# w2 of expert 5 loaded in two halves and w2 of expert 7 in 8, 4 and 4 rows, with the second products in the same pieces

## The chip, the cores and the metric

The kernel runs on one core of a Trainium2 chip. The metric is the device time of one execution in microseconds (us). Four runs of the kernel before gave 181.62 to 182.16 us, with a median of 181.73 us.

## The reference

Eight experts each apply a two-layer network to their own 256 tokens. x is 8 x 256 x 512, w1 is 8 x 512 x 2048, w2 is 8 x 2048 x 512, all float32; b1 and b2 are the biases.

```
h = np.matmul(x, w1) + b1[:, np.newaxis, :]
h = np.maximum(h, 0)
return (np.matmul(h, w2) + b2[:, np.newaxis, :]).astype(np.float32)
```

## The kernel before, in words

Everything is loaded into SBUF as float16 (the DMAs issued by GpSimd convert on the way) and multiplied by TensorE into float32 sums in PSUM.

**The tiles.** The weights of one expert are one tile each: w1 is 128 partitions x 4 rows x 2048, w2 is 128 partitions x 16 rows x 512 (`nJ` = 16 rows per partition). Each is 2 MB in SBUF and 4 MB in DRAM. Three w1 tiles and three w2 tiles exist at a time (`w1_pool`, `w2_pool`, L48 and L49), so a load waits until the product that used the same buffer three experts ago is done.

**The first product** of an expert (`first_product`, L114 to L136) has 16 blocks of four matmuls each (L121); ScalarE adds b1 and applies the maximum with zero (L128), and writes `hT`. In its middle VectorE transposes x of the next expert (`transposes`, L95).

**The second product** (`second_product`, L166 to L185) begins with two bias matmuls (L171), one for each block of 128 tokens. Then come 32 matmuls (L178), one for each of two token blocks (`tb`) and 16 rows (`j`) of w2, which sum up in the two PSUM tiles `po[0]` and `po[1]`. For the experts in `HALVED` (6 and 7) the 32 go in two halves: rows 0 to 7 for both token blocks, then rows 8 to 15 for both. For the others all 16 rows of one token block come first. `store` (L142) then copies `po[0]` out on VectorE (L156) and `po[1]` on ScalarE (L157).

**The order of the work.** The outer loop (L227) does at step s the first product of expert s and the second product of expert s - 3 (`LAG`). At the end, after the first product of expert 7, the second products of experts 4, 5, 6 and 7 follow each other; the last three have no first products between them. All weight loads are issued by GpSimd (POOL) from one list, `ring` (L215 to L225), in the order in which the products need them, and travel on one queue, q0. `load_w2` (L88 to L93) issues w2 of experts 0 to 5 as one DMA each and that of experts 6 and 7 as two DMAs of eight rows. PE and POOL keep the order in which the program is written (`ordered`).

**The stores.** The results of experts 0 to 3 and of experts 4 and 5 are collected in two group tiles (`GROUPS`) and stored by POOL with `flush` (L138, DMA at L140), behind the last weights on q0: 2 MB for the first group and 1 MB for the second. Expert 6's result is stored in three parts (`PARTS`, L164): rows 0 to 24 and 121 to 127 by SyncE (SP, queue q1), the 96 rows between by ScalarE (ACT, queue q10). Expert 7's result is one store by SP on q1, 0.5 MB.

Of the kernel before, what the change touches and what calls it, by code (L numbers as in the profile page):

```python
# [10 lines left out]
def kernel(  # L11
# [9 lines left out]
    nc = tc.nc  # L21
    fp32 = mybir.dt.float32
    fp16 = mybir.dt.float16
    E, T, H = x.shape
# [4 lines left out]
    nJ = M // P  # L29
# [4 lines left out]


    GROUPS = {0: 4, 4: 2}
    HALVED = (E - 2, E - 1)


    PARTS = {E - 2: ((0, 25, False), (25, 121, True), (121, 128, False))}  # L40
# [3 lines left out]
    def ordered(ins):  # L44
        return tc.keep_in_program_order(ins)
# [20 lines left out]
    w2_sb = [None] * E  # L66
# [2 lines left out]
    results = {}  # L69
    group_of = {first + i: (first, n) for first, n in GROUPS.items() for i in range(n)}  # L70

    def load_x(first, n):

        R = n * T // P
        t = x_pool.tile([P, R, H], fp16, tag=f"x{first}", name=f"x{first}")
        ordered(nc.gpsimd.dma_start(  # L76
            out=t, in_=x[first : first + n].rearrange("e (p r) h -> (e p) r h", r=R)
        ))
        for i in range(n):
            x16[first + i] = (t, i * (P // n), R)  # L80
# [7 lines left out]
    def load_w2(e):  # L88
        src = w2[e].rearrange("(p j) h -> p j h", j=nJ)
        w2_sb[e] = w2_pool.tile([P, nJ, H], fp16, tag="w2", name="w2sb")  # L90
        half = nJ // 2 if e in HALVED else nJ
        for lo in range(0, nJ, half):
            ordered(nc.gpsimd.dma_start(out=w2_sb[e][:, lo : lo + half], in_=src[:, lo : lo + half]))  # L93

    def transposes(e):  # L95

# [45 lines left out]
    def store(e, po):  # L142
        if e in group_of:
            first, n = group_of[e]
            split, rows = n, P // n
            if e == first:
                results[e] = group_pool.tile(
                    [P, split * nTB, H], fp32, tag=f"out{e}", name=f"out{e}")
        else:
            first, n, split, rows = e, 1, 1, P  # L150
            results[e] = out_pool.tile([P, nTB, H], fp32, tag="out", name="out")
        out_sb = results[first]
        at = (e - first) * rows
        for k in range(split):
            part = slice(k * rows, (k + 1) * rows)
            nc.vector.tensor_copy(out=out_sb[at : at + rows, k * nTB, :], in_=po[0][part])  # L156
            nc.scalar.copy(out=out_sb[at : at + rows, k * nTB + 1, :], in_=po[1][part])  # L157
        dst = out[first : first + n].rearrange("e (p r) h -> (e p) r h", r=split * nTB)
        if e in group_of:
            if e == first + n - 1:  # L160
                pending[first] = (dst, out_sb)
            return
        for p0, p1, scalar in PARTS.get(e, ((0, P, False),)):
            (nc.scalar if scalar else nc.sync).dma_start(out=dst[p0:p1], in_=out_sb[p0:p1])  # L164

    def second_product(e):  # L166
        po = []
        for tb in range(nTB):
            t = psum_o.tile([P, H], fp32, tag=f"po{tb}", name=f"po{tb}")
            po.append(t)  # L170
            ordered(nc.tensor.matmul(  # L171
                out=t, lhsT=ones1, rhs=b2_sb[0:1, e * H : (e + 1) * H], start=True, stop=False,
            ))
        half = nJ // 2 if e in HALVED else nJ
        for lo in range(0, nJ, half):
            for tb in range(nTB):
                for j in range(lo, lo + half):
                    ordered(nc.tensor.matmul(  # L178
                        out=po[tb],
                        lhsT=hT[e][:, j, tb * P : (tb + 1) * P],  # L180
                        rhs=w2_sb[e][:, j, :],
                        start=False,
                        stop=(j == nJ - 1),
                    ))
        store(e, po)  # L185

    x32 = []
    for e in range(nXF32):
# [4 lines left out]
        out=b2_sb,  # L193
        in_=b2.rearrange("e h -> (e h)").rearrange("(o f) -> o f", o=1),
# [12 lines left out]
    for b in range(nB):  # L207
        nc.vector.transpose(  # L208
            out=b1T[b * B : (b + 1) * B, nB - 1 - b : nB - 1 - b + nJ * B],
            in_=b1_rows.rearrange("r (i j) -> r j i", j=nJ),  # L210
# [5 lines left out]
    for s in range(1, E + LAG - 1):  # L216
        if s < E:
            if s in X_LOADS:
                ring.append((s - 2, load_x, (s, X_LOADS[s])))
            ring.append((s - 2, load_w1, (s,)))  # L220
        if s >= LAG:
            ring.append((s - 2, load_w2, (s - LAG,)))
    ring.append((E + LAG - 3, load_w2, (E - 1,)))
    for first, n in GROUPS.items():
        ring.append((first + n + LAG, flush, (first,)))  # L225

    for s in range(E + LAG):  # L227
        while ring and ring[0][0] <= s:
            _, put, args = ring.pop(0)
            put(*args)  # L230
        if s < E:
            first_product(s)
        if s >= LAG:
            second_product(s - LAG)
# [31 lines left out]
```

## Time and profile before

| what | value |
|---|---|
| median of four runs | 181.73 us |
| the profiled execution | 181.7 us |
| its span, first to last instruction | 179.9 us |
| mean granted TensorE clock | 0.948 |
| PE (matmuls) busy | 129.0 us, 72% |
| DVE / ACT / POOL busy | 87.8 / 70.6 / 13.5 us |
| moved by DMA, as counted at the destination | 40.56 MB, mean 225 GB/s |
| queue q0 | 38.35 MB, 96.4% of the 16 DMA engines' span |
| read from / written to DRAM | 71.39 / 4.19 MB |
| one w2 DMA of 2 MB, issue to landing | 47.1 us median |
| one w2 DMA of 1 MB, issue to landing | 23.9 us median |
| matmul at L178 | 379 ns median, x256 |

"Span" is the time between the first and last instruction in the trace; the execution's own time is 1.8 us longer. "Issue to landing" is the time from the issuing instruction to the arrival of the last byte; where transfers queue up behind each other it is mostly queueing time. "DMA share" in a stretch of time is the mean busy share of the 16 DMA engines; it can read a little over 1 where packets on one engine overlap. "Granted clock" is the share of TensorE's full clock that the chip allowed in that stretch. The chain of waits is followed back from the last instruction: at each step to what released it. The loads of float32 weights into float16 tiles show up at about half the GB/s of the stores, because bytes are counted at the destination.

### The profile page before, as it was taken

What the parts mean: (1) busy time and instruction counts of PE and PEld (TensorE: products, weight loads), DVE (VectorE), ACT (ScalarE), POOL (GpSimd) and SP (SyncE); (2) the same over time, 40 slices, a digit from 0 to 9 for tenths busy, and PEclk for the clock granted to TensorE, in tenths of its full rate; (3) what the DMA queues carried; (4) which work ended last, traced back from release to release, by engine and by line L of the source; (5) the groups of instructions that cost most, each with busy time, mean ns of one, the idle gap of its engine ahead of it and who ended that gap; (6) DMA issues with size and microseconds to landing.
All of it is one profiled execution on the core that took longest, in us unless ns stands there. A gap on an engine that the chain in (4) does not pass through costs nothing.

```text
span 179.9 us, 1958 instructions
## 1 busy us (share of the span) xinstructions
PE 129.0 (72%) x784; PEld 86.9 (48%) x784; DVE 87.8 (49%) x125; ACT 70.6 (39%) x151; POOL 13.5 (7%) x28
## 2 busy tenths in 40 slices
PE   0006099979599930999769593959499986999960
PEld 0004079979487410794369242934189432434420
DVE  1999931988000199999999998003300020301010
ACT  0000458979477050491279006940549020020010
POOL 7100000220201010001100001000200011010000
PEclk9999999999879996599999999999969997899998
DMA  6999999999999999899999999999998999999995
GB/s 214 252 229 195 233 214 194 233 228 204 213 229 199 213 233 219 189 233 226 219 197 233 219 193 230 229 200 211 233 219 189 233 209 208 217 213 220 358 413 224
DMA packets 3828, 40.56 MB, mean 225 GB/s; under 512 B 460, under 2 KB 476, under 8 KB 1132
## 3 DMA queue, kind: packets, MB, share of 16 engines
q0 software_dynamic: 3232, 38.35, 96.4%
q1 hardware_dynamic: 476, 1.70, 2.5%
q10 hardware_dynamic: 112, 0.39, 0.5%
q8 instruction: 6, 0.10, 0.2%
q14 instruction: 2, 0.02, 0.0%
HBM read 71.39 MB, written 4.19 MB: 420 GB/s over the span
## 4 chain that ended last, share of the span: by engine, by line
DMA 67%; PE 26%; POOL 2%; another core or an unknown queue 1%; issue 1%; ACT 0%; POOLq 0%
DMA w1sb<-in_w_dram 44%; DMA w2sb<-in_w_dram 23%; PE po L178 17%; PE ph L121 8%; PE po L171 1%; POOL w1sb L84 1%; ACT out L157 0%; POOL x L76 0%; POOL b_sb L192 0%; POOL b_rows L196 0%; POOLq L250 0%
## 5 line engine op out<-in xcount | busy, mean ns | idle before, releaser
L121 PE MATMUL ph<-xT,w1sb 128*128 128x256 f16 x512 | 66.6, 298 | 38.1 <-DMA w1sb<-in_w_dram 26.3
L121 PEld LDWEIGHTS <-w1sb 128*128 128x128 f16 x512 | 60.8, 148 | 44.8 <-DMA w1sb<-in_w_dram 36.4
L112 DVE STREAM_TRANSPOSE xT<-x 32x256 f16<-32x256 f16 (+1 forms) x64 | 53.0, 889 | 25.9 <-DMA x<-in_x_dram 18.1
L128 ACT ACTIVATE hT<-ph,b1T 128x256 f16<-128x256 f32 x128 | 56.6, 477 | 19.7 <-PE ph L121 19.5
L178 PE MATMUL po<-w2sb,hT 128*128 128x512 f16 x256 | 58.2, 387 | 6.6 <-DMA w2sb<-in_w_dram 6.6
L178 PEld LDWEIGHTS <-hT 128*128 128x128 f16 x256 | 25.3, 99 | 39.5 <-issue 12.0
L156 DVE COPY out<-po 32x512 f32<-32x512 f32 (+2 forms) x22 | 15.1, 687 | 54.4 <-PE po L178 54.2
L157 ACT COPY out<-po 32x512 f32<-32x512 f32 (+2 forms) x22 | 12.7, 579 | 63.8 <-PE po L178 63.6
L109 DVE STREAM_TRANSPOSE xT<-x 32x256 f16<-32x256 f16 x32 | 13.9, 436 | 0.5
L93 POOL DMA_DIRECT2D w2sb<-in_w_dram x10 | 5.3, 534 | 70.7 <-PE po L178 70.7
L84 POOL DMA_DIRECT2D w1sb<-in_w_dram x8 | 4.9, 612 | 65.2 <-PE ph L121 64.4
L128 ACT ACT_TABLE_LOAD x1 | 1.3, 1283 | 20.2 <-DVE b1T L208 20.2
L171 PE MATMUL po<-b_sb,ones 1*128 1x512 f16 x16 | 4.8, 379 | 0.0
L208 DVE STREAM_TRANSPOSE b1T<-b_rows 32x512 f32<-32x512 f32 x4 | 4.1, 1034 | 0.1
L201 DVE CAST x<-x 128x1024 f16<-128x1024 f32 x2 | 1.4, 694 | 3.2 <-DMA x<-in_x_dram 3.2
L140 POOL DMA_DIRECT2D out_dram<-out x2 | 1.1, 542 | 11.0 <-ACT out L157 11.0
L171 PEld LDWEIGHTS <-ones 1*128 1x128 f16 x16 | 0.9, 92 | 2.1 <-issue 2.1
L76 POOL DMA_DIRECT2D x<-in_x_dram x2 | 1.1, 552 | 0.0
L197 DVE MEMSET ones<- 1x128 f16 x1 | 0.2, 165 | 0.8 <-PEq L250 0.8
L196 POOL DMA_DIRECT2D b_rows<-in_b_dram x1 | 0.5, 515 | 0.0
L192 POOL DMA_DIRECT2D b_sb<-in_b_dram x1 | 0.5, 513 | 0.0
L250 POOL MEMSET const-float32-0.0<- 128x1 f32 x1 | 0.1, 98 | 0.2 <-issue 0.2
(3 smaller groups left out, 0.3 us busy)
## 6 DMA issues: line engine op xcount, KB each, us to landing
w1sb<-in_w_dram POOLq DMA_DIRECT2D x8, 2048.0 KB, 34.3
w2sb<-in_w_dram POOLq DMA_DIRECT2D x6, 2048.0 KB, 47.1
w2sb<-in_w_dram POOLq DMA_DIRECT2D x4, 1024.0 KB, 23.9
out_dram<-out POOLq DMA_DIRECT2D x1, 2048.0 KB, 26.7
x<-in_x_dram SPq DMA_DIRECT2D x2, 512.0 KB, 3.8
x<-in_x_dram POOLq DMA_DIRECT2D x1, 1024.0 KB, 30.2
out_dram<-out POOLq DMA_DIRECT2D x1, 1024.0 KB, 17.6
x<-in_x_dram POOLq DMA_DIRECT2D x1, 512.0 KB, 24.2
```

Of the source, the lines that this page charges most:

```text
L84: ordered(nc.gpsimd.dma_start(out=w1_sb[e], in_=w1[e].rearrange("(p kc) m -> p kc m", kc=nKC)))
L93: ordered(nc.gpsimd.dma_start(out=w2_sb[e][:, lo : lo + half], in_=src[:, lo : lo + half]))
L109: nc.vector.transpose(out=out[:, :, g, :, 0, :], in_=block[:, :, :, 0, :])
L112: nc.vector.transpose(out=out[:, tb, g], in_=block[:, tb])
L121: ordered(nc.tensor.matmul(out=ph, lhsT=w1_sb[e][:, kc, :].rearrange("p (q j) -> p q j", j=nJ)[:, :, j], rhs=xT[e][:, kc, :], start=(kc == 0),
L128: nc.scalar.activation(out=hT[e][:, j, :].rearrange("p (tb k i) -> p tb k i", tb=nTB, k=split), in_=ph.rearrange("p (tb i k) -> p tb k i", ...
L156: nc.vector.tensor_copy(out=out_sb[at : at + rows, k * nTB, :], in_=po[0][part])
L157: nc.scalar.copy(out=out_sb[at : at + rows, k * nTB + 1, :], in_=po[1][part])
L171: ordered(nc.tensor.matmul(out=t, lhsT=ones1, rhs=b2_sb[0:1, e * H : (e + 1) * H], start=True, stop=False,))
L178: ordered(nc.tensor.matmul(out=po[tb], lhsT=hT[e][:, j, tb * P : (tb + 1) * P], rhs=w2_sb[e][:, j, :], start=False, stop=(j == nJ - 1),))
L201: nc.vector.tensor_copy(out=t, in_=x32[e])
L208: nc.vector.transpose(out=b1T[b * B : (b + 1) * B, nB - 1 - b : nB - 1 - b + nJ * B], in_=b1_rows.rearrange("r (i j) -> r j i", j=nJ),)
```

## The change

Three places change; the rest of the kernel is the same text.

```
-    HALVED = (E - 2, E - 1)
+    PIECES = {E - 3: (8, 8), E - 2: (8, 8), E - 1: (8, 4, 4)}
...
+    def pieces(e):
+        at, spans = 0, []
+        for n in PIECES.get(e, (nJ,)):
+            spans.append((at, at + n))
+            at += n
+        return spans
+
...
     def load_w2(e):
...
-        half = nJ // 2 if e in HALVED else nJ
-        for lo in range(0, nJ, half):
-            ordered(nc.gpsimd.dma_start(out=w2_sb[e][:, lo : lo + half], in_=src[:, lo : lo + half]))
+        for lo, hi in pieces(e):
+            ordered(nc.gpsimd.dma_start(out=w2_sb[e][:, lo:hi], in_=src[:, lo:hi]))
...
     def second_product(e):
...
-        half = nJ // 2 if e in HALVED else nJ
-        for lo in range(0, nJ, half):
+        for lo, hi in pieces(e):
             for tb in range(nTB):
-                for j in range(lo, lo + half):
+                for j in range(lo, hi):
```

Expert 5's w2 is loaded by two DMAs of eight rows (1 MB each) instead of one of 16 rows, and its 32 matmuls go in two halves as those of expert 6 do. Expert 7's second half is divided once more, into two DMAs of four rows (0.5 MB each), and its last 16 matmuls into two groups of eight. Expert 6 stays as it was. There are two more DMAs in all; the number of matmuls is the same.

## The prediction

> **What bounds the kernel now.** I read the clock and span first (one core, 179.9 us, mean granted clock 0.948), then the page's slices, the chain that ended last, and then the DMA engines over the last microseconds, since the chain alone doesn't say whether its last steps are needed.
>
> The slices (40 of 4.5 us each, from the page):
>
> ```profile
> PE   0006099979599930999769593959499986999960
> ...
> PEclk9999999999879996599999999999969997899998
> DMA  6999999999999999899999999999998999999995
> GB/s 214 252 229 195 233 214 194 233 228 204 213 229 199 213 233 219 189 233 226 219 197 233 219 193 230 229 200 211 233 219 189 233 209 208 217 213 220 358 413 224
> ```
>
> The reader is to see that the DMA row is full from the second slice to the last but one, that the rate doubles only where float32 results leave, and that PE has gaps until slice 33 and none afterwards. PEclk is low in slices 33 and 34.
>
> The end of the chain of waits (start, length, what):
>
> ```profile
> 108.47 41.37 DMA w2sb<-in_w_dram
> 149.84 0.04 issue
> 149.88 8.75 PE po L178 x32
> 158.63 0.53 PE po L171 x2
> 159.16 7.01 PE po L178 x32
> 166.18 0.53 PE po L171 x2
> 166.71 7.03 PE po L178 x32
> 173.74 0.02 issue
> 173.76 0.59 ACT out L157
> ```
>
> Read alone it says: expert 5's w2 lands late, and then three second products run without a pause. That is the place the change aims at. But the chain stops at 174.35 and the span is 179.9; the stores fill the rest. So the last view is the tail in stretches of 0.5 us (columns: length, busy time and count of PE, PEld, DVE, ACT and POOL, clock, DMA share, GB/s):
>
> ```profile
> 176.00:176.50 0.50, 0.00 (x0) 0.00 (x0) 0.00 (x0) 0.00 (x0) 0.00 (x0) 1.00 1.03 434
> 176.50:177.00 0.50, 0.00 (x0) 0.00 (x0) 0.00 (x0) 0.00 (x0) 0.00 (x0) 1.00 0.95 393
> 177.00:177.50 0.50, 0.00 (x0) 0.00 (x0) 0.00 (x0) 0.00 (x0) 0.00 (x0) 1.00 0.75 303
> 177.50:178.00 0.50, 0.00 (x0) 0.00 (x0) 0.00 (x0) 0.00 (x0) 0.00 (x0) 1.00 0.68 279
> 178.00:178.50 0.50, 0.00 (x0) 0.00 (x0) 0.00 (x0) 0.00 (x0) 0.00 (x0) 0.74 0.27 107
> 178.50:179.00 0.50, 0.00 (x0) 0.00 (x0) 0.00 (x0) 0.00 (x0) 0.00 (x0) 0.50 0.02 8
> ```
>
> The 16 DMA engines are full up to 177.0 and then fall idle one after another until about 178.6. There is no hole in which they wait for the last result. Two cuts of the DMA view by queue say why. From 175.7 to 177.4:
>
> ```profile
> q0 software_dynamic: 59, 0.36, 50.5%
> q1 hardware_dynamic: 77, 0.29, 42.3%
> ```
>
> and from 177.42 on:
>
> ```profile
> q1 hardware_dynamic: 62, 0.21, 19.9%
> ```
>
> q0 carries the weights and the two group stores; q1 is SP's queue, at this point expert 7's store, issued at 174.37. An engine that has emptied q0 finds its share of that store already waiting: with a gap the DMA share would dip between 175.5 and 177.0, and it reads 1.01, 1.03 and 0.95. **So the bound is the load of the DMA engines, from the first weights to the last store**, and PE's last 2 us are hidden behind group stores.
>
> **The change, part by part.** Landing times are issue time plus time to landing, from the DMA view cut around each issue: w2 of expert 3 at 64.88 + 56.0 = 120.88, w1 of 7 at 81.51 + 49.0 = 130.51, w2 of 4 at 89.15 + 51.0 = 140.15, w2 of 5 at 108.47 + 41.37 = 149.84, the halves of 6 at 128.25 + 26.5 = 154.75 and 128.78 + 30.8 = 159.58, those of 7 at 147.56 + 16.9 = 164.46 and 148.09 + 21.4 = 169.49. A whole transfer therefore takes (149.84 - 120.88) / 3 = 9.65 us, the first pair of halves 9.74, the second 9.91.
>
> *Removed on PE.* Expert 5's first half lands at 140.15 + 4.87 (the mean of the steps 4.91, 4.83 and 4.88) = 145.0. Its bias products start at 147.19 and the body follows 0.54 later (158.56 to 159.10 in expert 6), so 147.73 in place of 149.88: the 2.09 us wait goes. The clock fall goes too, I think: after the stretch 147.2 to 150.9, with PE busy 1.61 of 3.70 us, the granted clock was 0.51 from 150.9 to 154.4, and the product took 8.75 us instead of 7.07.
>
> *What is late next.* One matmul is 7.07 / 32 = 0.221 us, eight rows on both blocks 3.54, four rows 1.77. Expert 5 runs 147.73 to 151.27 and, its second half being there at 149.9, to 154.80. Expert 6 starts at 155.34 (first half 154.8), stops at 158.88 and waits 0.8 for its second half (159.67), to 163.21. Expert 7 is ready at 163.75, waits 0.8 for its first half (164.55), ends it at 168.09, finds rows 8 to 11 (167.0), ends them at 169.86, and finds the last four (169.65), to 171.63. PE ends 2.1 us earlier than 173.74. Behind each added wait stand only that expert's matmuls, the next bias pair and the copies; I priced them with it. The last copy and SP's store come 2.1 us earlier too.
>
> *What that is worth at the end: nothing.* Expert 7's store then meets q0's last group store sooner; on each engine its packets go ahead of some of flush(4)'s, and those end later by as much. Expert 6's store, 3 us earlier, trades places likewise: it waited 3.6 us behind q0 (only q0 packets between 166.8 and 170.4). If it now slips between the last w2 pieces, it delays them by at most its own 0.52 MB / 420 GB/s = 1.25 us, and PE would end by 172.9, still ahead of 173.74. The stage's own cover is large: it is the engines' work, up to about 178.6.
>
> *POOL.* Two more DMA issues of 0.53 us (L93: 534 ns mean). They lie in POOL's waits of 18 to 19 us, with over 20 us of transfers queued ahead. The second group of issues moves flush(0) from 148.60 to about 149.1, while q0 doesn't reach it before about 167. Pieces reuse completion semaphores eight transfers old; the third piece of 7 thus waits for w1 of expert 7, landed at 130.5. Cost nothing; if a cover failed it would be 0.5 us each.
>
> *Added on the bound: smaller packets.* The bytes stay, the pieces grow by two. Splitting a whole transfer costs 9.74 - 9.65 = 0.09 by the first pair, 0.26 by the second, and -0.10 if the quickest halves (2 x 4.83) stand beside the slowest whole (9.76). I take 0.09, since the second pair has expert 6's store issued beside it. For the quarter, the load of x for experts 2 and 3 has the same 0.5 MB and 4 KB per partition: it landed at 3.47 + 24.2 = 27.67, 2.47 us after w1 of expert 1 (2.90 + 22.3 = 25.2). Two of those against one half: 4.94 - 4.87 = 0.07, with the same bounds. Sum: 0.09 + 0.07 = **+0.16 us**, bounds -0.2 and +0.52.
>
> A rule speaks against the change here. The rows just given put an extra piece at under 0.1 us while the queue is full. The Trainium skill, "DMA: Bandwidth & Descriptors", section "Anatomy of one DMA", gives each SWDGE transfer a fixed cost of about 2.0 us beside its bytes; charged on the path, two more pieces would be 4.0 us and the time 185.7. I go by the rows: halves land 4.87 apart and leave no room for 2 us.
>
> **Sum.** The profiled execution took 181.7 us (span 179.9 and 1.8 around it), 0.03 under the median of 181.73. 181.70 + 0.16 = **181.86 us**, +0.07%.
>
> **Rivals.** *PE sets the end* (0.05): the chain of waits read at its word. Then expert 7's store lands 2.1 us earlier and the time is 179.6. For it: the store issued at 174.37 lands last, 4.6 us later. Against it: no idle DMA before 177.0. *The engines finish more evenly* (0.07): shares after 177.0 add up to (0.75 + 0.68 + 0.27 + 0.02) x 0.5 = 0.86 us, so with even loads they would end at 177.86 and not 178.6, up to 0.75 us less, about 181.1. For it: stores of 25, 96 and 7 rows load engines unevenly, and earlier ones mix differently. Against it: which engine carries which rows isn't changed.
>
> *Slower: pieces cost more on the full engines* (0.14): if the second pair's 0.26 is the price of a piece, the two add 0.52, 182.2. Place: q0, from 149.84 to the end, where every engine's delay goes straight to the last store. It decides from 0.18 per piece (0.36 us in all). For it: 9.91. Against it: 9.74, and the pair of x-sized steps.
>
> *The pieces don't free the matmuls singly* (a step inside my forecast): if the product still waited for the whole tile, PE would start at 149.9 as now and the time would be the same 181.86. Only the trace could tell.
>
> **How the numbers follow.** A measurement of this kernel tells about 0.2% (0.36 us) from no change. My forecast, with the main case from 181.5 to 182.1, has 0.74; the two faster cases 0.12, the slower 0.14. The range 181.2 to 182.3 adds the nearer parts of these, with the bounds -0.2 and +0.52 of the packet cost.
>
> **What would show it.** Right: expert 5's product starting near 147.8 at full clock, waits of about 0.8 us before the second half of 6 and the first of 7, the last matmul near 171.6, and yet DMA full until 177 and a span of 179.7 to 180.3. Wrong: a span that shortens with PE's end, or a dip of the DMA share between 172 and 177; a last w2 piece landing after 170.2 for the packet cost.

## The result, and the profile after

The changed kernel takes 182.21 us (median of 50 runs) where the kernel before takes 181.69 us (75 runs on the same chips): ratio 1.0024, 95% interval 1.0018 to 1.0031. It is slower by about a quarter of a per cent, although TensorE finishes earlier. The profiled execution took 182.14 us, with a span of 180.3 us.

From the page of the changed kernel, the slices again (40 of 4.5 us):

```profile
PE   0006199979599930999769994959499999988820
...
PEclk9999999999879996699978999999969999999985
DMA  5998998999999999999999999999999999999994
GB/s 214 252 233 191 233 218 189 233 231 218 194 233 198 213 229 229 214 196 233 229 203 207 233 218 196 225 229 214 196 233 198 218 214 213 220 214 200 371 414 202
```

The gap of PE in slice 33 is gone and so is the low clock in slices 33 and 34; instead PE now has small gaps in slices 35 to 37. The DMA row is full to the end as before. Where PE waits at the end, from the timeline of the changed kernel (start, length, what, and in brackets the idle time before and what ended it):

```profile
147.52 7.08 PE L183 MATMUL po<-w2sb,hT 128*128 128x512 f16 x32
...
155.06 3.63 PE L183 MATMUL po<-w2sb,hT 128*128 128x512 f16 x16
...
159.46 3.61 PE L183 MATMUL po<-w2sb,hT 128*128 128x512 f16 x16 [0.77 <-DMA w2sb<-in_w_dram]
...
164.32 5.34 PE L183 MATMUL po<-w2sb,hT 128*128 128x512 f16 x24 [0.72 <-DMA w2sb<-in_w_dram]
...
170.47 1.89 PE L183 MATMUL po<-w2sb,hT 128*128 128x512 f16 x8 [0.81 <-DMA w2sb<-in_w_dram]
```

Expert 5 starts at 147.5 without a wait, and the wait comes back in three parts of about 0.8 us. PE ends at 172.4 in place of 173.7, and SP issues expert 7's store at 173.0 in place of 174.4. And still the span is 0.4 us longer.

The tail of the changed kernel in stretches of 0.5 us shows only a little of it (DMA share and GB/s are the last two columns):

```profile
177.00:177.50 0.50, 0.00 (x0) 0.00 (x0) 0.00 (x0) 0.00 (x0) 0.00 (x0) 0.50 0.84 344
177.50:178.00 0.50, 0.00 (x0) 0.00 (x0) 0.00 (x0) 0.00 (x0) 0.00 (x0) 0.50 0.72 295
178.00:178.50 0.50, 0.00 (x0) 0.00 (x0) 0.00 (x0) 0.00 (x0) 0.00 (x0) 0.50 0.49 197
178.50:179.00 0.50, 0.00 (x0) 0.00 (x0) 0.00 (x0) 0.00 (x0) 0.00 (x0) 0.50 0.02 8
```

The engines are busier after 177.0 (0.84, 0.72, 0.49 and 0.02, against 0.75, 0.68, 0.27 and 0.02), but the last packet is over in the same stretch. Expert 7's store lands 6.1 us after its issue at 173.0, at 179.1; before it landed 4.6 us after 174.37, at 179.0. **So only 0.1 us of the 0.4 lies in the last landing. The rest comes after the last byte.** One has to look at the closing instructions of the kernel, which the groups and the chain leave out: the instructions of the line that launches the kernel. Of before, and then of after, the closing drains of POOL and SP (count, duration in ns as least/median/most, first and last start):

```profile
L261 POOLq DRAIN  x3: 45/97/18678, 160.1 to 179.6; - x3
L261 SPq DRAIN  x3: 7/7/7, 179.1 to 179.4; - x3
```

```profile
L266 POOLq DRAIN  x3: 45/97/23501, 156.1 to 180.1; - x3
L266 SPq DRAIN  x3: 7/7/7, 179.2 to 179.8; - x3
```

POOL's first drain begins when it issues its last store (`flush(4)`, for experts 4 and 5) and is the long one: before it ended at 160.1 + 18.7 = 178.8, after at 156.1 + 23.5 = 179.6. That store's landing, from the DMA view cut around its issue, first of before (issued at 160.13), then of after (issued at 156.10):

```profile
out_dram<-out POOLq DMA_DIRECT2D x1, 1024.0 KB, 17.6
```

```profile
out_dram<-out POOLq DMA_DIRECT2D x1, 1024.0 KB, 22.4
```

It landed at 177.7 to 177.8 before and at 178.5 after, and the drain ended 1.0 to 1.1 us later both times. SP's drain, which follows the landing of expert 7's store by 0.1 us, started at 179.1 and 179.2. The kernel ends 0.7 to 0.8 us after the later of the two: SP's before (179.1), POOL's after (179.6).

The DMA view by queue shows how little of the group store (on q0) was late. From 177.42 on, q1 alone moved packets before, as the prediction shows; in the changed kernel q0 still had six packets left:

```profile
q1 hardware_dynamic: 77, 0.26, 22.3%
q0 software_dynamic: 6, 0.01, 0.8%
```

Expert 7's store (on q1) did not run ahead of it as a whole: it was issued at 173.0, but between 173.4 and 176.0 the view shows packets of q0 alone, and from 175.7 to 177.4 q1 moved 0.25 MB where it moved 0.29 MB before. So an earlier issue went together with a later end of the group store, but the order of the two stores' packets on a single DMA engine isn't shown.

### The profile page after: what moved, and what is told of

Its sections match the earlier page's. It is cut to its first block, busy times and chain, and to the rows that moved or that the text cites. A ratio compares the mean times of both kernels' runs of the same rounds, so it can differ in the third digit from the quotient of the medians.

```text
span 180.3 us, 1960 instructions
## 1 busy us (share of the span) xinstructions
PE 128.8 (71%) x784; PEld 87.0 (48%) x784; DVE 87.9 (49%) x125; ACT 70.8 (39%) x151; POOL 14.5 (8%) x30
## 4 chain that ended last, share of the span: by engine, by line
DMA 58%; PE 20%; DVE 13%; issue 2%; ACT 1%; POOL 1%; another core or an unknown queue 0%; DVEq 0%; ACTq 0%
DMA w1sb<-in_w_dram 27%; DMA x<-in_x_dram 19%; PE ph L127 14%; DMA w2sb<-in_w_dram 12%; DVE xT L115 6%; PE po L183 5%; DVE xT L118 5%; DVE b1T L213 2%; DVE x L206 1%; ACT L134 1%; POOL w2sb L99 1%; ACT out L163 0%; PE po L177 0%; POOL w1sb L91 0%; ACT hT L134 0%
## 5 line engine op out<-in xcount | busy, mean ns | idle before, releaser
L127 PE MATMUL ph<-xT,w1sb 128*128 128x256 f16 x512 | 67.8, 301 | 38.1 <-DMA w1sb<-in_w_dram 26.3
L183 PE MATMUL po<-w2sb,hT 128*128 128x512 f16 x256 | 56.9, 379 | 5.5 <-DMA w2sb<-in_w_dram 5.5
L183 PEld LDWEIGHTS <-hT 128*128 128x128 f16 x256 | 24.8, 98 | 37.4 <-issue 9.3
L99 POOL DMA_DIRECT2D w2sb<-in_w_dram x12 | 6.4, 535 | 70.1 <-PE po L183 70.1
```

The costliest lines, as they stand in the source:

```text
L99: ordered(nc.gpsimd.dma_start(out=w2_sb[e][:, lo:hi], in_=src[:, lo:hi]))
L127: ordered(nc.tensor.matmul(out=ph, lhsT=w1_sb[e][:, kc, :].rearrange("p (q j) -> p q j", j=nJ)[:, :, j], rhs=xT[e][:, kc, :], start=(kc == 0),
L183: ordered(nc.tensor.matmul(out=po[tb], lhsT=hT[e][:, j, tb * P : (tb + 1) * P], rhs=w2_sb[e][:, j, :], start=False, stop=(j == nJ - 1),))
```

## The experiments

Two theories stood against each other. **Theory 1, the drain:** expert 7's store, issued earlier, gets ahead of a part of the last group store on the DMA engines; that store lands later, and POOL's closing drain needs about another 1.1 us after it. **Theory 2, dear pieces:** the rival "slower" of the prediction; each extra piece costs about 0.2 us on the full engines. Ratios are to the kernel before on the same chip. "Store" below is the issue of expert 7's store.

**Loads alone.** Pieces in the loads, but each group of products begins with its last row, so that PE waits as before.

```
-                for j in range(lo, hi):
+                for j in reversed(range(lo, hi)):
```

(For expert 5 the group is all 16 rows and for expert 7 its halves, from a second table that isn't printed here; the loads keep their pieces.)

> The loads go in the pieces of the changed kernel, but the products of experts 5 and 7 begin each group with its last row, so that they wait for the later piece as in the kernel before. Theory 1 (drain): POOL's closing drain ends about 1.0 us after its last store has landed, and the kernel ends with the later of that drain and SP's last store; it became the later one because expert 7's store got ahead of it. Here that store is issued at 174.3 to 174.6 as before, so the drain ends before SP's last store lands, and only the packet cost of 0.1 us is left: ratio 1.0003 to 1.0009. Theory 2 (dear pieces): each extra piece costs about 0.2 us on the full DMA engines, with or without the products: ratio 1.0020 to 1.0028.

Measured 0.9997, interval 0.9987 to 1.0006. The store was issued at 174.0. The pieces alone cost no time that can be measured, and theory 2's 1.0020 is excluded.

**Each half of the change alone.**

```
+    PIECES = {E - 3: (8, 8), E - 2: (8, 8), E - 1: (8, 8)}
```

> Only expert 5's w2 is in halves; expert 7 stays in two halves. Theory 1 (drain): PE ends near 173.1 and expert 7's store is issued about 0.6 us earlier than before; a part of its packets gets ahead of the last group store, and the drain moves by some tenths: ratio 1.0003 to 1.0018. Theory 2 (dear pieces): one extra piece, 0.2 us: ratio 1.0009 to 1.0015. The trace tells more than the time here: by theory 1 POOL's drain ends about 1.0 us after the last group store landed, and the span follows the later of the two ends.

Measured 1.0000 (0.9991 to 1.0009), a little under what theory 1 gave. PE didn't end at 173.1 in the profiled execution but at 173.7, and the store was issued at 174.4, not earlier than before; SP's drain (179.2) was the last. PE had waited 2.2 us for expert 7's second half, which landed at 170.1. Expert 6's store was issued as early as in the changed kernel (163.7), so that alone doesn't make the loss.

```
+    PIECES = {E - 2: (8, 8), E - 1: (8, 4, 4)}
```

> Only expert 7's second half is divided; expert 5 is one load and one product. PE stays without a pause from 149.9 on and ends near 173.7, as before. Theory 1 (drain): expert 7's store is issued at 174.4 as before, the drain stays ahead of SP's last store, and 0.05 us of packets are left: ratio 0.9998 to 1.0008. Theory 2 (dear pieces): one extra piece, 0.2 us: ratio 1.0009 to 1.0015.

Measured 1.0011 (1.0000 to 1.0022): by its time alone this fits theory 2 better. The trace tells why my number for theory 1 was off. After the same wait for expert 5 the clock did not fall this time, so PE ended at 171.7 and not at 173.7, the store was issued at 172.3, and POOL's drain ended at 179.7, after SP's at 179.1:

```profile
L266 POOLq DRAIN  x3: 45/92/21617, 158.0 to 180.2; - x3
L266 SPq DRAIN  x3: 7/7/7, 179.1 to 179.9; - x3
```

SP's end is that of before, so in this execution no dear piece sits on the engines, and the longer span is the drain's. It is one of the two slowest of twelve (182.23 us, median 181.90), so it doesn't tell how much of the median's loss is the drain's.

**An earlier store without any piece.** The kernel before, with 8 of expert 7's matmuls left out; a kernel that does less.

```
-                for j in range(lo, lo + half):
+                for j in range(lo, 12 if e == E - 1 and lo else lo + half):
```

(The `stop` flag of the last matmul moves to row 11 with it, here and in the next kernel.)

> The kernel before, all loads as before, but expert 7's last four rows of w2 aren't multiplied (8 of its 32 matmuls are left out, and its output is incomplete). PE ends 1.8 us earlier, near 172.0, and expert 7's store is issued near 172.6. No piece is added. Theory 1 (drain): the earlier store alone makes the kernel slower, though it does less work: the last group store lands later, POOL's drain ends near 179.6, ratio 1.0015 to 1.0028, span near 180.3. Theory 2 (dear pieces): nothing is added, 0.9995 to 1.0005 or faster.

Measured 1.0019 (1.0000 to 1.0037), median 182.00 against 181.75. The store was issued at 172.4, and POOL's drain ended at 158.6 + 20.8 = 179.4, after SP's 179.3:

```profile
L261 POOLq DRAIN  x3: 45/97/20836, 158.6 to 179.9; - x3
L261 SPq DRAIN  x3: 7/7/7, 179.3 to 179.7; - x3
```

Doing less made it no faster, and in the median slower, as theory 1 says; theory 2 has nothing to add there. With the store held back by three more copies:

```
-            nc.scalar.copy(out=out_sb[at : at + rows, k * nTB + 1, :], in_=po[1][part])
+            for _ in range(4 if e == E - 1 else 1):
+                nc.scalar.copy(out=out_sb[at : at + rows, k * nTB + 1, :], in_=po[1][part])
```

> The same with 8 matmuls left out, but ScalarE's copy of expert 7's second block made four times, so that the store is issued near 174.4 again. Theory 1 (drain): back to the time before, ratio 0.9995 to 1.0006. Without the drain the added copies change nothing against the same kernel without them, or make it slower.

Measured 1.0012 (0.9996 to 1.0029), the median equal to that of before (181.75). Store at 174.1, POOL's drain at 178.8, SP's at 179.1. The direction is theory 1's, but the intervals of the two runs overlap.

**The changed kernel with a later store.** The same repeated copy, three times and four times in all, with all pieces in place, and the changed kernel beside the second.

> The changed kernel, with ScalarE's copy of expert 7's second block made three times, so that the last store is issued about 1.3 us later, near 174.3, though all loads and products go in pieces. Theory 1 (drain): the last group store lands earlier than in the changed kernel, POOL's drain ends before 179.1, and the later store costs nothing: faster than the changed kernel, ratio to before 1.0003 to 1.0012, span near 180.0. Theory 2 (dear pieces): as the changed kernel, 1.0024, or slower because of the added copies.

Measured 1.0008 (0.9997 to 1.0020); store at 174.1, POOL's drain at 178.8, SP's at 179.0, span 179.8. That is within theory 1's band. But the profiled execution (181.61 us) is among the fastest of the twelve; their median, 181.87, is still 0.25 us above that of the kernel before on the same chip (181.62), and no trace shows what those 0.25 us are.

> The changed kernel with the copy made four times, the store issued near 174.8. Theory 1 (drain): POOL's drain is out of the way in nearly all executions, only the pieces' 0.1 us is left: ratio 1.0002 to 1.0010, faster than the changed kernel beside it. Theory 2 (dear pieces): 1.0024 or more.

> The changed kernel itself, on the chip of the other three: 1.0018 to 1.0031 by both theories, as measured already. It is there for the direct comparison with the late store.

Measured 1.0016 (1.0005 to 1.0027), median 181.96, against 1.0023 (1.0005 to 1.0040), median 182.22, for the changed kernel itself. Extra work on ScalarE makes the kernel 0.26 us shorter in the medians; the intervals overlap. In the later store's profile POOL's drain (179.3) is before SP's (179.5), but SP's itself is 0.4 us later than before, which goes with 1.0016 in place of the 1.0010 at most that I expected. The store was issued at 175.2 there, 0.8 us later than before; whether that delay did it isn't shown.

**The drain by itself.** The kernel before, with expert 7's store issued by POOL.

```
-            (nc.scalar if scalar else nc.sync).dma_start(out=dst[p0:p1], in_=out_sb[p0:p1])
+            issuer = nc.gpsimd if e == E - 1 else nc.scalar if scalar else nc.sync
+            issuer.dma_start(out=dst[p0:p1], in_=out_sb[p0:p1])
```

> The kernel before, with expert 7's store issued by POOL instead of SP, as the last transfer on q0. Theory 1 (drain): the last landing stays near 179.0, but POOL's drain now follows it by 1.0 us, where SP's last wait needed 0.1: slower by 0.8 to 1.0 us, ratio 1.0044 to 1.0058, and the trace shows the drain ending 1.0 us after the landing. Without such a drain the time would be that of before, 0.9995 to 1.0010, since the issue is 0.5 us long and the engines are still full.

Measured 1.0037 (1.0024 to 1.0050), median 182.52 against 181.67: 0.85 us slower, in the expected band by the medians and a little under it by the ratio. The store, issued at 174.18, landed 4.8 us later at 179.0, where SP's had landed; the drain went on to 174.2 + 5.8 = 180.0:

```profile
L262 POOLq DRAIN  x3: 45/92/5836, 174.2 to 180.5; - x3
```

Same bytes, same landing, another queue: that is the price of the drain.

**The last group store moved to SP,** behind expert 7's store, in the changed kernel and in the kernel before.

```
+        if e == E - 1:
+            last_dst, last_src = pending.pop(4)
+            ordered(nc.sync.dma_start(out=last_dst, in_=last_src))
```

(`flush(4)` leaves POOL's list, and SP's stores keep the program's order; neither is printed here.)

> The changed kernel, with the last group store (experts 4 and 5) issued by SP behind expert 7's store, so that POOL's last transfer is the first group store, which lands near 175.4. Theory 1 (drain): POOL's drain ends near 176.5 and decides nothing; SP's last store lands near 179.1 as the engines' load has it: ratio to before 1.0003 to 1.0010, span near 180.0, 0.35 us less than the changed kernel. Theory 2 (dear pieces): the pieces are all there, 1.0020 to 1.0028.

> The kernel before with the same move of the last group store to SP, behind expert 7's store. There the drain was not the last to end, so by theory 1 little changes: 0.9990 to 1.0010 if the engines stay full; but q0 is empty from about 173 on and the two stores are only issued at 174.4 and 174.8, so some engines may wait up to 2 us, and then it is slower, up to 1.010. Theory 2 says nothing of it. Beside the changed kernel with the same move it tells whether the earlier results are worth something once the drain is out of the way.

Measured 1.0017 (1.0001 to 1.0033) and 1.0018 (1.0000 to 1.0036). POOL's drain ended at 176.7 and 177.6 and decided nothing, but the stores came too late for the engines. The medians, 181.99 and 182.05, don't tell the two apart, so the earlier results were worth nothing that can be measured here either. Of the kernel before with this move, the tail in stretches of 1 us (an execution of 182.78 us, one of the two slowest of twelve):

```profile
173.00:174.00 1.00, 0.86 (x4) 0.19 (x2) 0.00 (x0) 0.10 (x1) 0.00 (x0) 1.00 0.76 315
174.00:175.00 1.00, 0.00 (x0) 0.00 (x0) 0.00 (x0) 0.48 (x1) 0.00 (x0) 1.00 0.27 107
175.00:176.00 1.00, 0.00 (x0) 0.00 (x0) 0.00 (x0) 0.00 (x0) 0.00 (x0) 1.00 0.68 270
```

With q0 run dry, the share falls to 0.27: this is what a hole looks like, and the kernel before has none. In the changed kernel with the move the same stretches read 0.86, 0.80 and 0.95. So this pair doesn't isolate the drain. The first of the two came out above its expectation, though its interval reaches into it; I take the idle engines to be the reason.

**Many pieces.** w2 of experts 0 to 5 in halves too, products as before.

```
-        half = nJ // 2 if e in HALVED else nJ
+        half = nJ // 2
```

(in `load_w2` alone)

> The kernel before, with w2 of experts 0 to 5 loaded in halves too: six extra pieces on the full engines, all products as before. Theory 1 (drain) takes 0.05 us per piece from the steps between the pieces' completions in the trace: 0.3 us in all, ratio 1.0012 to 1.0022. Theory 2 (dear pieces): 0.2 us per piece, 1.2 us in all, ratio 1.0050 to 1.0080.

Measured 1.0035 (1.0017 to 1.0052), median 182.14 against 181.67: 0.47 / 6 = 0.08 us per piece by the medians, 0.11 by the ratio, between 0.05 and 0.16 by the interval. That is above theory 1's band and below theory 2's; the price I had taken in the prediction, 0.07 to 0.09, fits.

All profiled executions side by side (us from the span's start):

| kernel | expert 7's store issued | SP's drain starts | POOL's drain ends | span |
|---|---|---|---|---|
| before | 174.4 | 179.1 | 178.8 | 179.9 |
| loads alone | 174.0 | 179.1 | 178.9 | 179.9 |
| expert 5 alone | 174.4 | 179.2 | 178.9 | 180.0 |
| later store, 3 copies | 174.1 | 179.0 | 178.8 | 179.8 |
| rows left out, later store | 174.1 | 179.1 | 178.8 | 179.9 |
| many pieces | 173.7 | 179.3 | 179.2 | 180.1 |
| later store, 4 copies | 175.2 | 179.5 | 179.3 | 180.3 |
| changed | 173.0 | 179.2 | 179.6 | 180.3 |
| changed, again | 173.3 | 179.4 | 179.7 | 180.4 |
| expert 7 alone | 172.3 | 179.1 | 179.7 | 180.4 |
| rows left out | 172.4 | 179.3 | 179.4 | 180.2 |
| store on POOL | 174.2 | 179.1 | 180.0 | 180.7 |
| group store on SP, changed | 173.3 | 179.4 | 176.7 | 180.2 |
| group store on SP, before | 174.5 | 180.2 | 177.6 | 181.0 |

In every row the span is 0.7 to 0.8 us after the later of the two ends. Where POOL still has the last group store and SP expert 7's, POOL is last if that store was issued at 173.3 or earlier, and SP is last if it was issued at 173.7 or later. The step between shows too: the last group store landed at 178.4 to 178.6 in the four profiles with the early store and at 177.7 to 178.2 in the seven others. No experiment pointed to a version faster than both kernels: the best, the loads alone, equals the kernel before.

## Why the prediction was right, and where it was not

The number held by luck. I forecast +0.16 us and the medians differ by 0.52; 182.21 lies outside my main case (181.5 to 182.1) and inside the range only because its upper part, up to 182.3, was there for dear pieces, which the loads alone exclude.

- *The DMA engines are the bound.* Right: PE ended 1.4 us earlier and gained nothing, and the engines stayed full up to 177.
- *PE's new course.* Right up to the last piece: start at 147.5 (147.7 forecast), full clock, waits of 0.77 and 0.72 (0.8 and 0.8). The last four rows landed at 170.4, not at 169.65. I had named a landing after 170.2 as a sign that the packet cost is wrong; it isn't one. With the loads alone, the same pieces, the last landed at 169.5, and there expert 6's store was issued at 166.5 as before. In the changed kernel that store, issued at 163.7, slipped in between the last pieces, as I had allowed for with up to 1.25 us; PE ended at 172.4, within the 172.9 of that case.
- *Packets.* Right in size: 0.1 us in the last landing, about 0.1 us per piece in the kernel with many pieces. The 185.7 us that a full charge for each extra transfer would have made didn't come: the two more pieces of the loads alone cost at most 0.1 us.
- **The step that failed: "What that is worth at the end: nothing."** I wrote that expert 7's packets go ahead of some of `flush(4)`'s "and those end later by as much", and took the exchange as free. The bytes to move are indeed the same, but the two stores don't count alike at the end: SP's closing drain follows the landing of its store by 0.1 us, POOL's ends 1.0 to 1.1 us after the landing of its own. I had called the cover large; it was 0.3 us (178.8 against 179.1 before), and the end of POOL's drain moved by 0.8 us. In the profiled execution that is 179.6 - 179.2 = 0.4 us, to which the packets' 0.1 comes; the term I had at zero was the larger one.
- *The rivals.* "Slower" came true with another mechanism than the one I gave. Dear pieces are excluded by the loads alone (at most 1.0006), so a mechanism that I hadn't named gave the time that I had put under this rival. "PE sets the end" and "more even engines" didn't show.
- *What stays open.* By the times the effect of the drain is 0.2 to 0.3 us, near the resolution of single comparisons: holding the store back gave 0.25 and 0.26 us in the medians of two pairs, but the intervals of each pair overlap. In all fourteen profiles the span follows the later of the two closing ends; the times alone would not have proved it. With the store held back the changed kernel still had medians 0.21 and 0.25 us above the kernel before, about half of the loss, and what that is stays open: the pieces by themselves don't cost it. How the early issue delays the last packets of the group store isn't shown either. Why SP's own end lay 0.2 to 0.4 us later in the changed kernel's second profile and with four copies isn't settled; the engines' last ends differ that much between executions.

## What to carry to other kernels

Here the DMA engines were full to the end, and an earlier result brought no time; it only moved the ends of the last stores, and then it mattered which queue ended last. So look at the closing drains, not only at the landings. Where it can be had without idle engines, give the last bytes to the queue that closes fastest, here SP's, and let POOL's last transfer land at least 1 us sooner. And before you remove a wait at the end of the compute, look for a hole in the tail of the transfers: without one, as here, the wait was worth nothing.

## What the runs showed of the hardware

- POOL's closing drain ended 1.0 to 1.3 us after the landing of its last transfer in all fourteen profiles, while SP's closing wait took 0.1 us.
- A store on SP's or ACT's queue didn't start at once beside a full q0: only q0 packets moved for 3.6 us after expert 6's store was issued in the kernel before, and in the changed kernel expert 7's store, issued at 173.0, moved nothing between 173.4 and 176.0.
- The fall of TensorE's clock after a wait is not the same in each execution. After a wait of 2.1 us for expert 5 the granted clock was 0.51 from 150.9 to 154.4 in the kernel before (10 matmuls in 3.5 us); with expert 7 alone changed, PE was busy for the same 1.61 of 3.70 us before that stretch, and the clock was 1.00 in it (18 matmuls). Of six profiles with such a wait before a whole product, the product took 8.6 to 8.8 us in three and 7.1 us in three. The issue of expert 7's store moves with it: 174.4 in the first of these two executions, 172.3 in the second. How often each comes in one kernel isn't shown.
